# Block products for the short sequence's gate columns, with its normalised sums of x made early

## The chip, the core and the metric

The kernel runs on one core of a Trainium2 chip. The metric is the device time of one execution in microseconds. All matrix products are done on TensorE (PE) with each fp32 operand split in two parts, a high one and a low one, so that one logical product is three matmuls: high x high, high x low, low x high.

## The reference, cut to what matters

Two sequences, one of 1024 tokens (the short one, sequence 0) and one of 2048 (the long one, sequence 1, worked on in two chunks of 1024), get 16 meta tokens in front and pass through one encoder layer. What matters here is the input projection and what is made of its gate columns:

```python
xn = _rmsnorm(h, g_pre)                  # one norm per token
proj = xn @ w_in + b_in                  # 1024 -> 6672 columns
na_q, na_k, na_v, na_z, ml_qk, ml_v, ml_z, ml_o, ml_g, mg = jnp.split(proj, SPLIT_IDX, axis=-1)
ya = (neighbourhood_attention(na_q, na_k, na_v) * silu(na_z)) @ w_a
yb = (mlstm(ml_qk, ml_v, ml_g, ml_o) * silu(ml_z)) @ w_b
ga, gb = jnp.split(jax.nn.sigmoid(mg), 2, axis=-1)      # the 2048 gate columns
y = (ga * ya + gb * yb) @ w_out
return h + _rmsnorm(y, g_post)
```

The gate columns `mg` are 16 blocks of 128 columns. They are needed only at the end, when the two branches are merged.

## The kernel before, in words

**Two streams of work, one order on PE.** `dense()` (L1993) yields the projections, and at the end the merge and output products, piece by piece, each with a planned cost in us: 0.235 for a matmul 512 wide, 0.12 for one 256 wide (L134). `sparse()` (L2038) yields the steps of the mLSTM and of the attention. `run()` (L2057) interleaves them: each sparse step names how much dense work is to stand beside it (L135: 0.965 for an attention step of the long sequence), and the dense generator is drawn on until that sum is used up. So PE's order is written out by hand; the other engines' order comes from a scheduler, apart from side work that is put behind the last evacuation.

**The dense order** is `PLAN` (L42). The short sequence's `m` columns (mLSTM), then its `n` and `v` columns (attention), then the long sequence's two chunks, then the `n` and `g` columns of both long chunks, then the short sequence's `g` columns, then six final blocks of 512 tokens (`final`, L1825): merge products, then output products. The sparse order is mLSTM 0, attention 0, mLSTM 1, attention 1.

**Direct columns.** A block of 128 columns for 512 tokens is 8 steps of k with three matmuls 128x512 each, 24 in all (`fm_half`, L707, and `mm3`, L199 to L204). Columns and tokens of a chunk of 1024 give 2 x 24 per block of columns. Three PSUM banks (`pj`) take such results in turn.

**Block products.** For the chunks in `SW` (L43, the two long chunks) the columns `n` and `g` are made in pairs of blocks: the 2 x 2 block product (two column blocks by two halves of tokens, with k split in two) is done with seven products instead of eight (`sgates`, L923). A product is 4 steps of k by three matmuls, 12 matmuls (L955 to L957). It needs sums and differences of the weight blocks (made by `wprep`, L567, and `nprep`, L600) and of blocks of x (made by `tprep`, L627), both split in two parts again and kept in DRAM. `tprep` reads x's two halves of tokens from SBUF, adds their parts, and writes four tiles of sums `t0` to `t3`; `tload` (L901) reads them back for `sgates`. While a chunk's sums are being loaded, its first two pairs are done as direct columns (`lead`, L835). In `sgates` three banks A, E, R change roles: ACT copies a bank into another (L972, L979) or into SBUF (L981), DVE adds such a copy to a bank (L985, L987), and the result goes to `fm_evac` (L657).

**Normalisation.** For the long sequence x is normalised when it is split (`build_half`, L466). For the short sequence it isn't: its projections start before the norms are known, and `fm_evac` multiplies each result by a row of norms `rr` on DVE (L669 to L672). `rr` is written to DRAM (L508) and read back in `gclose` (L899) for the gate columns much later. x of the short sequence, and of the long one's first chunk, is written to DRAM by a queue `xput` (`xkeep`, L540) and read back when its later columns come up.

**Side work.** `beside()` (L549) runs after each piece of dense work and counts these turns. It issues one write of `xput` at certain turns and advances each side generator at every n-th turn: `wprep` at every 3rd, at every 6th from its last two pairs on; `tprep` of the first long chunk at every 4th from the start of that chunk's `m` columns; `tprep` and `nprep` of the second at every 2nd. What is left of a `tprep` is run down before the chunk's last group of columns (`group`, L1000). A turn is six matmuls 512 wide or twelve 256 wide.

**Buffers.** SBUF has a left pool that is `bp` in most stages (work tiles, such as four `xr` of 128x1024) and is exchanged for `gp` (the tiles `t1` to `t3`) in the stage of block products (`gopen`, L887, and `gclose`, L893). A final block loads its y tiles with a generator (`yload`, L1784) into the buffers of x, and waits until the attention of its 512 tokens is done.

## Time and profile before

| | |
|---|---|
| runs of the kernel before | 2701.67 us median of 3 (2700.21 to 2706.63) |
| the profiled execution | 2705.33 us, of which 2703.3 is the span of the trace |
| mean granted clock of TensorE | 0.995 |
| matmuls | 16000 |
| bytes moved by DMA | 783.72 MB |

Times in the profile are those of one execution, counted from the start of its span. PE is TensorE's matmuls, PEld its weight loads, DVE the vector engine, ACT the scalar engine, POOL GpSimd, SP the queue that issues nearly all DMAs. Matmuls are pipelined: the next one starts before the last has ended, so durations add up to more than the busy time. In a group's row, the last part tells how long the engine had been idle just before these instructions and what ended most of it.

### The profile page before, as it was taken

What the parts mean: (1) busy time and instruction counts of PE and PEld (TensorE: products, weight loads), DVE (VectorE), ACT (ScalarE), POOL (GpSimd) and SP (SyncE); (2) the same over time, 40 slices, a digit from 0 to 9 for tenths busy, and PEclk for the clock granted to TensorE, in tenths of its full rate; (3) what the DMA queues carried; (4) which work ended last, traced back from release to release, by engine and by line L of the source; (5) the groups of instructions that cost most, each with busy time, mean ns of one, the idle gap of its engine ahead of it and who ended that gap; (6) DMA issues with size and microseconds to landing.
All of it is one profiled execution on the core that took longest, in us unless ns stands there. A gap on an engine that the chain in (4) does not pass through costs nothing.

```text
span 2703.3 us, 47407 instructions
## 1 busy us (share of the span) xinstructions
PE 2658.4 (98%) x16000; PEld 2345.6 (87%) x16000; DVE 1910.4 (71%) x5234; ACT 1418.5 (52%) x3350; POOL 17.4 (1%) x100
## 2 busy tenths in 40 slices
PE   9999998999999999999999999999999999999998
PEld 7898897789987999878888888888889888989888
DVE  5444687978648888446866767658478989897954
ACT  6322555565345654356655566555355655656521
POOL 0000000000000000000000000000000000000000
PEclk9999998999999999999999999999999999999999
DMA  9988887899986898798889988895769798998965
GB/s 373 344 323 316 306 302 277 295 348 345 317 270 228 295 349 298 248 305 259 262 288 329 368 288 258 282 344 189 219 221 303 250 312 257 309 294 262 333 230 202
DMA packets 405986, 783.72 MB, mean 290 GB/s; under 512 B 51472, under 2 KB 180448, under 8 KB 404208
## 3 DMA queue, kind: packets, MB, share of 16 engines
q1 hardware_dynamic: 404624, 778.01, 85.6%
q0 software_dynamic: 1120, 2.69, 0.4%
q8 instruction: 127, 2.08, 0.3%
q14 instruction: 115, 0.94, 0.1%
HBM read 531.66 MB, written 248.88 MB: 289 GB/s over the span
## 4 chain that ended last, share of the span: by engine, by line
PE 70%; DVE 6%; DMA 5%; ACT 2%; issue 1%; SPq 0%; DVEq 0%; ACTq 0%
PE pj L202 8%; PE pj L203 8%; PE pj L204 8%; PE pj L955 6%; PE pj L957 6%; PE pj L956 6%; PE pj L1898 3%; PE pj L1899 3%; PE pj L1900 3%; PE pj L762 3%; PE pj L763 3%; PE pj L764 3%; PE sm L1247 2%; PE tr L1232 2%; DMA stk<-nq 1%
## 5 line engine op out<-in xcount | busy, mean ns | idle before, releaser
L202 PE MATMUL pj<-xh,whi 128*128 128x512 f32 (+1 forms) x992 | 385.5, 389 | 2.7 <-ACT st L679 1.5
L203 PE MATMUL pj<-xl,whi 128*128 128x512 f32 (+1 forms) x992 | 375.3, 378 | 0.1
L204 PE MATMUL pj<-xh,wlo 128*128 128x512 f32 (+1 forms) x992 | 374.7, 378 | 0.2 <-DVE wlo L304 0.2
L762 PE MATMUL pj<-whi,xh 128*128 128x256 f32 (+1 forms) x1152 | 329.7, 286 | 0.0
L763 PE MATMUL pj<-wlo,xh 128*128 128x256 f32 (+1 forms) x1152 | 325.0, 282 | 0.6 <-DMA wlo<-wl 0.6
L764 PE MATMUL pj<-whi,xl 128*128 128x256 f32 (+1 forms) x1152 | 324.7, 282 | 0.0
L204 PEld LDWEIGHTS pj<-xh,wlo 128*128 128x128 f32 x992 | 188.0, 189 | 37.3 <-DVE wlo L304 0.4
L1898 PE MATMUL pj<-whi,mh 128*128 128x256 f32 x768 | 219.6, 286 | 0.7 <-DMA whi<-wh 0.7
L763 PEld LDWEIGHTS pj<-wlo,xh 128*128 128x128 f32 x1152 | 217.0, 188 | 1.0 <-DMA wlo<-wl 0.8
L202 PEld LDWEIGHTS pj<-xh,whi 128*128 128x128 f32 x992 | 188.2, 190 | 33.8 <-ACT st L679 2.0
L762 PEld LDWEIGHTS pj<-whi,xh 128*128 128x128 f32 x1152 | 217.1, 188 | 0.2
L764 PEld LDWEIGHTS pj<-whi,xl 128*128 128x128 f32 x1152 | 217.0, 188 | 0.0
L1900 PE MATMUL pj<-whi,mlo 128*128 128x256 f32 x768 | 216.4, 282 | 0.0
L1899 PE MATMUL pj<-wlo,mh 128*128 128x256 f32 x768 | 216.3, 282 | 0.0
L203 PEld LDWEIGHTS pj<-xl,whi 128*128 128x128 f32 x992 | 188.4, 190 | 28.9 <-issue 1.0
L202 PE MATMUL pj<-yh,whi 128*128 128x512 f32 x384 | 154.1, 401 | 0.0
L203 PE MATMUL pj<-yl,whi 128*128 128x512 f32 x384 | 150.8, 393 | 0.8 <-DVE yl L1800 0.8
L204 PE MATMUL pj<-yh,wlo 128*128 128x512 f32 x384 | 151.2, 394 | 0.0
L1898 PEld LDWEIGHTS pj<-whi,mh 128*128 128x128 f32 x768 | 145.2, 189 | 1.8 <-DMA whi<-wh 0.9
L1899 PEld LDWEIGHTS pj<-wlo,mh 128*128 128x128 f32 x768 | 145.4, 189 | 0.9
L1900 PEld LDWEIGHTS pj<-whi,mlo 128*128 128x128 f32 x768 | 145.3, 189 | 0.0
L1239 DVE TENSOR_TENSOR pts<-tr,pts 96x384 fp32r<-96x384 f32 (+2 forms) x192 | 118.7, 618 | 32.8 <-ACT pts L1234 31.1
(368 smaller groups left out, 6739.2 us busy)
## 6 DMA issues: line engine op xcount, KB each, us to landing
whi<-wh SPq DMA_DIRECT2D x136, 512.0 KB
wlo<-wl SPq DMA_DIRECT2D x136, 512.0 KB
whi<-q SPq DMA_DIRECT2D x63, 512.0 KB
wlo<-q SPq DMA_DIRECT2D x55, 512.0 KB
wraw<-wu SPq DMA_DIRECT2D x48, 512.0 KB
gt<-st SPq DMA_DIRECT2D x96, 256.0 KB
tg<-gt SPq DMA_DIRECT2D x96, 256.0 KB
wh<-whi SPq DMA_DIRECT2D x36, 512.0 KB
```

Of the source, the lines that this page charges most:

```text
L202: mm(out, ah, bh, start=start, stop=False)
L203: mm(out, ah, bl, start=False, stop=False)
L204: mm(out, al, bh, start=False, stop=stop)
L762: nc.tensor.matmul(o, xh, wh, start=k == 0, stop=False)
L763: nc.tensor.matmul(o, xh, wl, start=False, stop=False)
L764: nc.tensor.matmul(o, xl, wh, start=False, stop=k == KT - 1)
L955: mm(bank, w[:, 0, k], xh[:, k], start=fresh and k == 0, stop=False, skip_group_check=True)
L956: mm(bank, w[:, 0, k], xl[:, k], start=False, stop=False, skip_group_check=True)
L957: mm(bank, w[:, 1, k], xh[:, k], start=False, stop=k == 3, skip_group_check=True)
L1898: nc.tensor.matmul(o, mh[:, k, xs], wh, start=clear > 0 and k == 0, stop=False)
L1899: nc.tensor.matmul(o, mh[:, k, xs], wl, start=False, stop=False)
L1900: nc.tensor.matmul(o, ml[:, k, xs], wh, start=False, stop=clear < 2 and k == KT - 1)
```

## The change

- `SW` now has the short sequence's chunk too: of its eight pairs of gate columns the first two stay direct, the other six are made by seven products each. The plan's order stays.
- The short sequence's block sums are made early, during its own `m`, `n` and `v` columns, from turn 34 on, one step at every 6th turn. There `tprep` adds the two parts of x, multiplies by `rr`, splits the normalised x again, writes it to DRAM (in place of the unnormalised x that `xput` wrote), and makes the sums from it. The gate columns are then not multiplied by `rr` at the evacuation, and `rr` is not kept in DRAM any more.
- `wprep` no longer splits and writes the weight block "21" of the six pairs that are no longer direct anywhere.
- `tprep` of the first long chunk begins at turn 370 and steps at every 3rd turn.
- `xput` (now of the long chunk alone) writes at every 3rd turn from the start.
- The last pair's `sgates` starts the y loads of the first final block; the left pool is reopened as `bp` after the short sequence's gate columns instead of ahead of them.
- Dense work beside an attention step of the long sequence: 0.93 instead of 0.965.

The core of the diff:

```diff
-SW = ((1, 0), (1, 1024))
+SW = ((0, 0), (1, 0), (1, 1024))
...
-A_N, A_D, A_A, A_G = (1.08, 0.965), 1.63, 1.79, 1.3
+A_N, A_D, A_A, A_G = (1.08, 0.93), 1.63, 1.79, 1.3
...
-            self.xkeep(s, 0, self.xs[0], NM)
-            self.xkeep(s, t0, x)
...
-                self.RD = self.dp.tile([P, D], F32, name="rrd")
-                nc.sync.dma_start(self.RD[:, :], self.rr.rearrange("p a t -> p (a t)"))
...
-        if self.xput and self.turn > 36 and self.turn % (6 if self.turn < 280 else 3) == 1:
+        if self.xput and self.turn % 3 == 1:
...
-                nc.scalar.activation(o[:, :, 0], raw[:, f], AF.Copy)
-                sub(o[:, :, 1], raw[:, f], o[:, :, 0].bitcast(F32))
-                for q, op in enumerate(ops):
+                c = slice(p > 7 and ops[0] == "21", 2)
+                nc.scalar.activation(o[:, c, 0], raw[:, f, c], AF.Copy)
+                sub(o[:, c, 1], raw[:, f, c], o[:, c, 0].bitcast(F32))
+                for q, op in list(enumerate(ops))[c]:
...
-    def tprep(self, s, t0):
+    def tprep(self, s, t0, after):
...
-        while len(self.xs) < 2:
+        while len(self.xs) < 2 or self.turn < after:
             yield
-        (h0, l0), (h1, l1) = self.xs
+        if s == 0:
+            for a in range(2):
+                self.xkept[s, t0 + 512 * a] = [dp.tile([P, KT, 512], F32, name=f"x{part}{s}_{t0 + 512 * a}") for part in "hl"]
+        halves = [[x[:, :, b:b + 512].bitcast(F32) for x in y] for y, b in zip(self.xs, (0 if s else NM, 0))]
         for e in range(4):
             ks = slice(2 * e, 2 * e + 2)
             r0, r1, ta, hi = [self.bp.tile([P, 2, 512], F32, name="xr", bufs=4) for _ in range(4)]
-            for r, h, l in ((r0, h0, l0), (r1, h1, l1)):
-                nc.vector.tensor_tensor(r, h[:, ks, :512].bitcast(F32), l[:, ks, :512].bitcast(F32), op=ALU.add)
+            for a, (r, (h, l)) in enumerate(zip((r0, r1), halves)):
+                tt(r, h[:, ks], l[:, ks], ALU.add)
+                if s == 0:
+                    tt(r, r, self.rr[:, a:a + 1].to_broadcast([P, 2, 512]), ALU.mult)
                 yield
+            if s == 0:
+                for a, r in enumerate((r0, r1)):
+                    nc.scalar.activation(hi.bitcast(F32R), r, AF.Copy)
+                    tt(ta.bitcast(F32R), r, hi)
+                    for d, x in zip(self.xkept[s, t0 + 512 * a], (hi, ta)):
+                        nc.sync.dma_start(d[:, ks, :], x)
+                    yield
...
-            if s == 0:
+            if s == 0 and col < C_GA:
...
-        self.rr = self.bp.tile([P, 2, 512], F32, name="rr", tag="gain", bufs=1)
-        self.nc.sync.dma_start(self.rr.rearrange("p a t -> p (a t)"), self.RD[:, :])
...
-            if end and nxt:
-                nx = [self.xload(*nxt)]
+            if end and nxt[0] == "f":
+                self.ystart(*nxt[1:])
+                next(self.ygen)
+            elif end:
+                nx = [self.xload(*nxt[:2])]
...
-        if sw:
-            last = t0 > 0
-            self.sides.append([chain(self.tprep(s, t0), self.nprep() if last else ()), 2 if last else 4])
-            side_ = self.sides[-1]
+        if sw and not reuse:
+            self.tside = chain(self.tprep(s, t0, 34 if s == 0 else 370 if t0 == 0 else 0), self.nprep() if t0 else ())
+            self.sides.append([self.tside, 6 if s == 0 else 2 if t0 else 3])
...
-            if last and sw:
-                for _ in side_[0]:
+            if last and sw and (nxt or t0):
+                for _ in self.tside:
                     pass
...
-                for cost in self.sgates(s, t0, cols, self.lead(j), nxt and nxt[:2]):
+                for cost in self.sgates(s, t0, cols, self.lead(j), nxt):
                     yield cost
                     self.beside()
+                    if self.y:
+                        next(self.ygen, None)
+                        next(self.ygen, None)
```

More of the change, by code (lines that the diff above doesn't have):

```diff
@@ L545, in xkeep @@
                 d = self.dp.tile([P, KT, 512], F32, name=f"x{part}{s}_{t0}")
-                self.xput.extend((d[:, k, :], x[:, k, base:base + 512].bitcast(F32)) for k in range(KT))
+                self.xput.extend((d[:, k, :], x[:, k, :512].bitcast(F32)) for k in range(KT))
                 self.xkept[s, t0].append(d)
@@ L575, in wprep @@
             if p == 12:
-                self.sides[0][1] = 6
+                [x for x in self.sides if x[0] is self.wside][0][1] = 6
             raw = pool.tile([P, 2, 2, 512], F32, name="pr", bufs=1)
@@ L625, in nprep @@
                 yield
-    def tprep(self, s, t0):
+    def tprep(self, s, t0, after):
         nc, dp = self.nc, self.dp
-        self.TD[s, t0] = [[dp.tile([P, 4, 512], F32, name=f"t{j}{part}{t0}") for part in "hl"] for j in range(4)]
+        tt = lambda o, a, b, op=ALU.subtract: nc.vector.tensor_tensor(o, a, b, op=op)
+        self.TD[s, t0] = [[dp.tile([P, 4, 512], F32, name=f"t{j}{part}{s}{t0}") for part in "hl"] for j in range(4)]
         td = self.TD[s, t0]
-        while len(self.xs) < 2:
+        while len(self.xs) < 2 or self.turn < after:
             yield
-        (h0, l0), (h1, l1) = self.xs
+        if s == 0:
+            for a in range(2):
+                self.xkept[s, t0 + 512 * a] = [dp.tile([P, KT, 512], F32, name=f"x{part}{s}_{t0 + 512 * a}") for part in "hl"]
+        halves = [[x[:, :, b:b + 512].bitcast(F32) for x in y] for y, b in zip(self.xs, (0 if s else NM, 0))]
         for e in range(4):
@@ L1016, in group @@
             last = j == len(jobs) - 1
-            if last and sw:
-                for _ in side_[0]:
+            if last and sw and (nxt or t0):
+                for _ in self.tside:
                     pass
-                self.sides = [x for x in self.sides if x is not side_]
+                self.sides = [x for x in self.sides if x[0] is not self.tside]
             if last and sw and t0:
```

14 lines of the change are left out of this document (7 added, 7 removed).

## The prediction

> **What bounds the kernel now.** I read four views in this order: the page's engine table, its chain that ended last, the table of busy time in stretches of 50 us, and the instructions in order of time.
>
> ```profile
> span 2703.3 us, 47407 instructions
> PE 2658.4 (98%) x16000; PEld 2345.6 (87%) x16000; DVE 1910.4 (71%) x5234; ACT 1418.5 (52%) x3350; POOL 17.4 (1%) x100
> ...
> DMA packets 405986, 783.72 MB, mean 290 GB/s; under 512 B 51472, under 2 KB 180448, under 8 KB 404208
> ...
> PE 70%; DVE 6%; DMA 5%; ACT 2%; issue 1%; SPq 0%; DVEq 0%; ACTq 0%
> ```
>
> PE is idle for only 2703.3 - 2658.4 = 44.9 us and holds 70% of the chain. So a matmul taken out shortens the run, and anything that adds PE idle time lengthens it. The stretches (columns: PE, PEld, DVE, ACT, POOL busy, granted clock, DMA share, GB/s) show where this holds:
>
> ```profile
> 100.00:150.00 50.00, 50.00 (x397) 49.30 (x396) 18.61 (x29) 13.36 (x18) 0.00 (x0) 1.00 0.88 319
> ...
> 300.00:350.00 50.00, 48.53 (x312) 43.88 (x311) 37.63 (x94) 28.75 (x72) 3.79 (x15) 1.00 0.95 338
> 350.00:400.00 50.00, 50.00 (x429) 50.00 (x428) 43.20 (x131) 28.18 (x70) 0.10 (x1) 1.00 0.86 294
> ...
> 500.00:550.00 50.00, 45.60 (x216) 37.75 (x215) 41.22 (x137) 25.83 (x64) 0.10 (x1) 0.93 0.81 281
> ...
> 600.00:650.00 50.00, 49.49 (x410) 49.27 (x410) 46.17 (x151) 26.36 (x66) 0.10 (x1) 1.00 1.01 345
> ...
> 1850.00:1900.00 50.00, 50.00 (x260) 42.28 (x259) 36.52 (x135) 23.55 (x63) 2.39 (x8) 1.00 0.50 166
> ...
> 1950.00:2000.00 50.00, 50.00 (x259) 42.03 (x258) 34.44 (x89) 29.89 (x67) 0.00 (x0) 1.00 0.58 176
> ...
> 2250.00:2300.00 50.00, 48.73 (x247) 40.40 (x246) 48.05 (x123) 25.96 (x59) 0.00 (x0) 1.00 0.89 277
> ```
>
> The short sequence's gate columns run from about 1796 to 2010 us. PE is full there, DVE has 30% and the DMA engines 42 to 50% to spare.
>
> **What a matmul is worth.** Multiplying by its listed duration is the trap here, so its row comes first, then starts of matmuls in the gate stage (the first pair, direct) and in the block products just before it (the second pair).
>
> ```profile
> L202 PE MATMUL pj<-xh,whi 128*128 128x512 f32 x824 | 337.0, 409 | 1.5 <-ACT st L679 1.5
> ```
> ```profile
> 1905.66 0.39 PE L202 MATMUL pj<-xh,whi 128*128 128x512 f32 x1
> ...
> 1911.91 0.39 PE L202 MATMUL pj<-xh,wlo 128*128 128x512 f32 x1
> ```
> ```profile
> 1788.15 0.39 PE L955 MATMUL pj<-xh,wlo 128*128 128x512 f32 x1
> ...
> 1793.68 0.39 PE L955 MATMUL pj<-xh,wlo 128*128 128x512 f32 x1
> ```
>
> One lasts about 0.39 to 0.41 us, but the next starts long before it ends: 27 matmuls lie between the first pair, 6.25 / 27 = 0.2315 us each, and 24 between the second, 5.53 / 24 = 0.2304. Spacing, not duration, is what PE's time is made of.
>
> The Trainium skill, "TensorE: Matmul & The Clock Gate", section "Wait — 56ns, not 53.3ns?", gives warm starts N / 2.4 GHz + 2.5 ns apart, 215.7 ns for N = 512. By that figure the 72 matmuls counted below would be worth 15.5 us; this trace's spacing is 7% wider, and the trace decides.
>
> **The change part by part.**
>
> *Removed from PE.* Of the eight pairs of gate columns (16 columns of 128), the first two stay direct: 2 pairs x 2 columns x 2 halves x 8 k-steps x 3 = 192 matmuls. The other six were 6 x 2 x 2 x 24 = 576 and become 6 pairs x 7 products x 12 = 504. That is 72 fewer, 576 x 0.2315 - 504 x 0.2304 = 133.3 - 116.1 = 17.2 us by the two spacings, or 72 x 0.231 = 16.6 by their mean. I take **-16.7 us**.
>
> *The gate stage around it.* The 32 products with the row of norms at the evacuation go (DVE, 0.70 us each, 22 us in all); 12 sums and 18 copies of a bank come.
>
> ```profile
> L672 DVE TENSOR_TENSOR pj<-pj,rr x88: 415/699/700, 26.9 to 2008.7; 128x512 f32<-128x512 f32 x67, 128x248 f32<-128x248 f32 x11, 128x264 f32<-128x264 f32 x10
> ```
> ```profile
> L985 DVE TENSOR_TENSOR st<-pj,st 128x512 f32<-128x512 f32 x26 | 17.9, 687 | 10.6 <-PE pj L957 7.2 <-DMA wlo<-q3s 3.3
> L979 ACT ACTIVATE pj<-pj 128x512 f32<-128x512 f32 x26 | 15.1, 582 | 22.4 <-PE pj L957 22.4
> ```
> ```profile
> PE pj L955 <- ACT pj L972: 1.4, 2, 0.7
> PE pj L202 <- ACT st L679: 1.5, 1, 1.5
> ```
>
> DVE's balance here is 12 x 0.69 - 22 = -14 us; ACT gains 18 x 0.58 = 10 us beside PE. In the 26 pairs that already run this way the bank copies held PE for 1.4 us in two waits, both on the first copy of a chunk, so one more chunk costs about 0.7. All three banks are in use in this scheme, and a bank copy has to be done within one product (12 x 0.2304 = 2.8 us), where direct columns leave two banks spare. The 26 pairs ran mostly beside the mLSTM; these six run mostly beside the attention, for which no row exists. Bounds 0 and 6 x 1.5 = 9 (the longest wait of a dense matmul for ACT, once a pair); I take +1, near the 0.7.
>
> *Data.* Six more units of DMA appear: block sums of x, 32 writes of 256 KB (8 MB) and 8 MB read back; weights, 25 units of 1 MB where there were 16, so +9 MB; six 0.5 MB weight blocks are no longer written. The sum is about +22 of 784 MB. The read-back and the weights fall into the gate stage with its DMA share of 0.50 to 0.58: I count 0. If that cover were gone, an extra 17 MB at 290 GB/s would be 59 us of transfers, spread over some 200 us.
>
> *Sums of the short x, made early.* One step every sixth turn of the dense stream from turn 36; 36 steps end at turn 246. Counting turns by the columns' yields, these are about 65 and 372 us. The steps issue, by the rows below: DVE 8 sums, 8 scalings, 8 splits and 4 wide lows at 1.22, and 16 block sums and 8 narrow lows at 0.68, together 28 x 1.22 + 24 x 0.68 = 50 us; ACT 12 x 1.06 + 8 x 0.63 = 18 us; SP 48 issues where the old write-back of x had 32.
>
> ```profile
> L639 DVE TENSOR_TENSOR xr<-xh,xl x16: 1210/1218/1226, 496.2 to 904.0; 128x1024 f32<-128x1024 f32 x16
> L641 DVE TENSOR_TENSOR xr<-xr x8: 681/684/694, 504.7 to 911.0; 128x512 f32<-128x512 f32 x8
> L649 ACT ACTIVATE xr<-xr x24: 611/627/1060, 529.6 to 924.6; 128x512 fp32r<-128x512 f32 x16, 128x1024 fp32r<-128x1024 f32 x8
> ```
>
> A step is 1.4 us of DVE in 8 us. At 100 to 150 us DVE is at 37% and takes that unseen. At 350 to 400 it is at 86% and the last three steps still come, so the cover ends there. Behind a step that waits for its buffer's write to land stand the evacuations, and for those the matmuls; with three banks a direct column outlasts about 2 x 24 x 0.231 = 11 us. The longest such hold on the chain now is:
>
> ```profile
> 841.45 7.05 DMA t1h<-xr
> ```
>
> That is under 11, so I take 0, with a bound of one full PE stall above (6.8, priced next).
>
> *Sums of the long x, moved later.* Their 28 steps (per quarter 9 DVE and 3 ACT instructions and 8 writes) begin at turn 370, about 590 us, instead of near 490, and are moved past the write-back of the long x and the weight preparation on SP. What they leave is a stall:
>
> ```profile
> 496.17 1.21 DVE L639 TENSOR_TENSOR xr<-xh,xl 128x1024 f32<-128x1024 f32 x1
> ...
> 498.23 1.22 DVE L639 TENSOR_TENSOR xr<-xh,xl 128x1024 f32<-128x1024 f32 x1
> ...
> 504.65 0.68 DVE L641 TENSOR_TENSOR xr<-xr 128x512 f32<-128x512 f32 x1
> ...
> 509.06 0.45 PE L202 MATMUL sm<-v,sh 128*128 128x130 f32 x1 [4.40 <-DVE num L1688]
> ```
> ```profile
> 510.00:515.00 5.00, 5.00 (x16) 4.01 (x16) 4.97 (x25) 2.26 (x7) 0.05 (x1) 0.62 0.42 129
> 515.00:520.00 5.00, 5.00 (x27) 4.22 (x26) 4.86 (x19) 3.53 (x9) 0.05 (x1) 1.00 0.43 162
> ```
>
> PE waits 4.40 us for an mLSTM result that DVE reaches late, and three of these sums (3.1 us) stand in DVE's line ahead of it. Then the granted clock is 0.62 for a stretch: 16 matmuls in place of 27, about 2.4 us lost. So one such stall is 4.4 + 2.4 = 6.8 us. Without the three sums the wait would be 1.3 us and the clock might stay up: 3.1 + 2.4 = 5.5 won. The other bound is 0: what is late next is the mLSTM's own line on DVE, 82% busy there. I take **-3**. Where the steps go, at 600 to 650 us, DVE is at 92% and the DMA share 1.01, but about as many of the same steps are there already: 0 to +1, taken as 0.
>
> The Trainium skill, the same page, section "What's actually happening", says that the PE clock halves after an idle window of about 3.4 us and needs a busy one to return. The 4.40 us wait and the 0.62 behind it agree; the rule speaks against this change wherever it makes a new wait of that length.
>
> *Pace and end.* The attention's dense filler falls from 0.965 to 0.93 per step; with 541 steps that is 18.9 of the planner's us against 72 x 0.235 = 16.9 of filler that no longer exists. It matters:
>
> ```profile
> L1264 DVE TENSOR_TENSOR yg<-yg,zt x24: 671/681/693, 843.3 to 2591.8; 128x512 f32<-128x512 f32 x24
> ...
> L203 PE MATMUL pj<-yl,whi x64: 387/390/504, 2603.3 to 2647.8; 128*128 128x512 f32 x64
> ```
>
> The short stretch between the last attention product (2591.8) and the last block's first matmul (2603.3) is one store, one load and one split: the end now hangs on the attention and on the dense stream alike. With 16.7 us less dense work and the old pace, dense would be there at 2586.6, before the attention had ended, and PE would wait. With the new pace the attention ends 18.9 x 0.231 / 0.235 = 18.6 us sooner too, near 2573, and the gap is kept. I count 0; if the attention couldn't be pressed together the whole gain would go (a rival below).
>
> *Small edits, one answer.* The row of norms is no longer stored and reloaded (two 0.5 MB transfers), half of ACT's and DVE's share of six weight blocks goes (6 x 0.6 us each), and the left pool is reopened after these columns, just ahead of the last product blocks: their first gate loads can then wait for the block sums' last reader, one product (2.8 us) before the end, while two spare banks give 5.5 us. 0, with a bound of +2.
>
> **Sum.** -16.7 (matmuls) + 1 (bank copies) - 3 (the stall) = -18.7 us. The profiled execution took 2705.3 (2703.3 of span and 2.0 around it), so 2686.6; it lies 3.7 above the median 2701.67 of the runs shown, so on that scale the forecast is **2683**.
>
> **Rivals.** (Times on the scale of the median.)
>
> *More is won.* The 4.4 us stall goes with its slow stretch and the copies cost nothing: -17.2 - 6.8, 2678. For it: 3.1 of the 4.4 us are named above. Against: the rest of DVE's line is still there.
>
> *Less is won.* The bank copies, now beside the attention's ACT work, hold PE by 1.5 us a pair, and the stall stays: -16.7 + 9, 2694. For it: the slack of one product, and PE idle 1.3 us at 2250 to 2300 with DVE at 96%. Against: PE at 100% in all of 1850 to 2000 with the attention already there.
>
> *The pace doesn't hold.* DVE at 96% (2250 to 2300) can't bring the attention to an end sooner; the last block starts at 2603 as now, and only the stall's 3 us are won: 2699. Against: DVE is at 96% in a few stretches only, and pressing the attention's 541 steps into 18.6 of some 715 us less raises its share by under 3%.
>
> *Slower.* The place is 300 to 408 us, where the short sequence's mLSTM begins and DVE is already at 75 to 86%. If the early sums slip, because a step waits for its buffer's write, their steps of 1.4 us in 8 (17%) lie on top of 86% and DVE is full; each mLSTM step that comes 4 us late then costs 6.8 us, as at 509. Three of them give 20.4 and undo the gain; five give 34: -16.7 + 1 - 3 + 34, 2717. It decides from a slip of about ten turns, 15 us, on. For it: waits like this already occur when x is built beside this mLSTM:
>
> ```profile
> 460.09 0.55 PE L1648 MATMUL sc<-q,kh 128*128 128x256 f32 x1 [4.31 <-DVE nwy L166]
> ```
>
> Against: 33 of the 36 steps are due before 350 us, where DVE has 25% or more to spare.
>
> A reading of 72 x 0.394 = 28.4 us, by duration, would give 2673; the spacing rules it out.
>
> **How the numbers follow.** Forecast 0.58, more 0.12, less 0.14, pace 0.08, slower 0.08. A measurement of this kernel can tell about 0.3% from no change, which is 8.1 us: faster means under 2693.6. The forecast and "more" lie below it, "less" sits on the line and is split 0.08 to 0.06, "pace" is within. Faster 0.78, same 0.14, slower 0.08. The range takes the forecast, "more" and "less" with some play beyond them, 2674 to 2697; the two cases above it are 0.16 together.
>
> **What would show it.** Right: 15928 matmuls in place of 16000; the group of 128x512 direct products down by 576 and the block products up by 504, with spacing still 0.231; PE's busy time down by about 17 us and its idle time no higher than 44.9; no sums of x between 480 and 590 us and a shorter wait, or a clock of 1.00, near 509; the last attention product near 2573 and the last block's first matmul 10 to 15 us behind it. Wrong: PE waits for ACT's bank copies of more than 1 us in the gate stage, stretches with the clock under 1.00 between 300 and 420, DVE waits for the writes of the block sums, or a wait of PE ahead of the last block. If matmul busy time fell by 17 us and the span didn't, the lost time must stand in one of these waits.

## The result

The changed kernel takes **2713.85 us** (median of 20 runs, 2704.46 to 2721.22), the kernel before 2702.64 in 20 runs beside it (2696.68 to 2712.44): a ratio of 1.0038, 95% interval 1.0028 to 1.0048. It is 11.2 us slower where 18.7 us of gain were forecast, and it lies above the range. The profiled execution took 2712.26 us, with a mean granted clock of 0.992 (0.995 before). The head of its page:

```profile
span 2710.5 us, 47460 instructions
PE 2645.7 (98%) x15928; PEld 2334.1 (86%) x15928; DVE 1937.3 (71%) x5266; ACT 1440.0 (53%) x3388; POOL 16.9 (1%) x100
...
DMA packets 411652, 805.75 MB, mean 297 GB/s; under 512 B 52016, under 2 KB 180992, under 8 KB 409104
...
PE 84%; DMA 6%; DVE 6%; ACT 2%; issue 1%; SPq 1%; DVEq 0%; ACTq 0%
```

The work did go: 72 matmuls fewer and 12.7 us less of PE's busy time (matmuls at half clock count as longer, and about 41 us of the span are at half clock where it was 25). But PE's idle time rose from 44.9 to 2710.5 - 2645.7 = 64.8 us, and the DMAs grew by 22 MB, as counted. The stretches that answer to those shown of before (PE, PEld, DVE, ACT, POOL, granted clock, DMA share, GB/s), and in a second block two of the kernel before, from 450 and 1900 us on:

```profile
300.00:350.00 50.00, 46.02 (x293) 41.59 (x292) 40.46 (x92) 27.86 (x68) 3.31 (x14) 0.97 0.91 324
450.00:500.00 50.00, 40.74 (x187) 33.66 (x187) 41.86 (x107) 36.34 (x85) 0.30 (x3) 0.86 0.92 326
500.00:550.00 50.00, 48.88 (x246) 40.74 (x246) 42.53 (x137) 29.65 (x72) 0.10 (x1) 1.00 0.84 286
1900.00:1950.00 50.00, 46.85 (x219) 38.31 (x218) 17.81 (x59) 17.43 (x33) 2.38 (x8) 1.00 0.90 246
1950.00:2000.00 50.00, 50.00 (x246) 41.76 (x245) 28.53 (x77) 29.70 (x64) 0.00 (x0) 0.97 0.87 278
```
```profile
450.00:500.00 50.00, 45.69 (x214) 37.85 (x214) 42.64 (x103) 33.84 (x79) 0.20 (x2) 0.93 0.94 350
...
1900.00:1950.00 50.00, 50.00 (x230) 40.92 (x229) 22.07 (x63) 15.90 (x30) 0.00 (x0) 1.00 0.71 218
```

Read the third row of the change first: between 500 and 550 us PE is at 48.9 with a clock of 1.00, where before it had 45.6 and 0.93, so the stall at 505 us is gone as forecast. The loss is in the rows around it. At 450 to 500 PE has 40.7 us in place of 45.7 and a clock of 0.86 in place of 0.93, at 300 to 350 it has 46.0 in place of 48.5, and in the gate stage, at 1900 to 2000, the DMA share is 0.90 and 0.87 where it was 0.71 and 0.58. The longest waits of PE (what waits, on what; us in all, times, longest):

```profile
PE sc L1658 <- DVE q L1612: 12.4, 2, 11.0
...
PE tr L1789 <- DVE hb L1784: 3.2, 1, 3.2
PE pj L963 <- ACT pj L990: 3.2, 1, 3.2
```

The order of matmuls on PE is the same in both kernels up to the short sequence's gate columns, so each matmul can be compared with itself. By the time of the kernel before, after minus before is -1.6 us at 116 us, +6.5 at 338, +11.3 at 418, +17.8 at 447, +5.1 at 542, +14.5 at 888 and +16.9 at 1804, just ahead of the gate columns. So it is lost before the changed products run, in two places: up to 470 us, of which 5.1 us are left at 542, since the kernel before has stalls of its own in between, and between 542 and 888. In the second place PE waits 3.0 us for ACT at 792, and 2.8 and 2.3 us for DVE at 835 and 839, with a slow stretch behind the first and the last; DVE is busy for all of 830 to 835 there, while the DMA share is 0.14. After 1804 the change wins 9.7 us back, down to the 7.2 by which the two spans differ, though three more stalls (1945, 2006 and 2025 us) stand there.

**The stall at 448 us.** Instructions in order of time on PE, with what the engine waited for in brackets, then those of ACT and DVE ahead of it:

```profile
447.84 0.39 PE L204 MATMUL pj<-xh,wlo 128*128 128x512 f32 x1
459.26 0.58 PE L1658 MATMUL sc<-q,kh 128*128 128x256 f32 x1 [11.02 <-DVE q L1612]
```
```profile
446.26 0.42 ACT L1638 ACTIVATE v<-va 128x260 fp32r<-128x260 f32 x1 [4.11 <-DMA va<-mv]
```
```profile
453.38 3.49 DVE L531 TENSOR_TENSOR xl<-xt,xh 128x1024 fp32r<-128x1024 f32 x3
...
457.65 1.21 DVE L567 TENSOR_TENSOR po<-pr,po 128x1024 fp32r<-128x1024 f32 x1
458.79 0.41 DVE L1612 TENSOR_TENSOR q<-cv,q 128x256 fp32r<-128x256 f32 x1
```

DVE is the engine named, and it is busy; but it started late. Ahead of it, ACT sat idle for 4.11 us until a load of the mLSTM (`va<-mv`) had landed. The splits of the long x (L531) then stand ahead of the one product that PE needs. The chain that ended last shows how far back this goes (start, us, what):

```profile
387.26 5.38 DMA t3h<-xr
...
394.52 4.67 DMA q<-whi
...
413.71 7.66 DMA xt<-xt
...
425.08 5.53 DMA va<-mv
...
434.92 5.77 DMA wraw<-wu
440.75 5.48 DMA va<-mv
```

In 59 us, up to 446, the chain passes through these six transfers and one stretch of PE, 9 us from 403.6 on. The first of them is a write of the block sums that the change makes early (`t3h`).

**The stall at 1945 us.** ACT, then PE, in the changed kernel:

```profile
1943.15 0.63 ACT L1177 ACTIVATE qB<-stk 64x512 fp32r<-64x512 f32 x1 [5.35 <-DMA stk<-nq]
...
1947.86 0.57 ACT L990 ACTIVATE pj<-pj 128x512 f32<-128x512 f32 x1
```
```profile
1948.48 0.50 PE L963 MATMUL pj<-xh,wlo 128*128 128x512 f32 x1 [3.15 <-ACT pj L990]
```

The long attention begins here. ACT's first instruction for it waits 5.35 us for the attention's first load, and the bank copy of the new products stands behind that in ACT's line. From its issue to its first use the load takes 7.9 us (1935.2 to 1943.2); in the kernel before it takes 4.7 (1916.9 to 1921.6).

### The profile page after: what moved, and what is told of

Its sections match the earlier page's. It is cut to its first block, busy times and chain, and to the rows that moved or that the text cites. A ratio compares the mean times of both kernels' runs of the same rounds, so it can differ in the third digit from the quotient of the medians.

```text
span 2710.5 us, 47460 instructions
## 1 busy us (share of the span) xinstructions
PE 2645.7 (98%) x15928; PEld 2334.1 (86%) x15928; DVE 1937.3 (71%) x5266; ACT 1440.0 (53%) x3388; POOL 16.9 (1%) x100
## 4 chain that ended last, share of the span: by engine, by line
PE 84%; DMA 6%; DVE 6%; ACT 2%; issue 1%; SPq 1%; DVEq 0%; ACTq 0%
PE pj L202 9%; PE pj L203 9%; PE pj L204 9%; PE pj L963 7%; PE pj L965 7%; PE pj L964 7%; PE pj L772 4%; PE pj L774 4%; PE pj L773 4%; PE pj L1908 3%; PE pj L1910 3%; PE pj L1909 3%; PE sm L1257 2%; PE tr L1242 2%; DMA xt<-xt 1%
## 5 line engine op out<-in xcount | busy, mean ns | idle before, releaser
L202 PE MATMUL pj<-xh,whi 128*128 128x512 f32 (+1 forms) x896 | 346.3, 387 | 2.0 <-ACT whi L303 2.0
L203 PE MATMUL pj<-xl,whi 128*128 128x512 f32 (+1 forms) x896 | 337.9, 377 | 0.1
L204 PE MATMUL pj<-xh,wlo 128*128 128x512 f32 (+1 forms) x896 | 337.6, 377 | 0.3 <-DVE wlo L304 0.3
L204 PEld LDWEIGHTS pj<-xh,wlo 128*128 128x128 f32 x896 | 170.4, 190 | 33.2 <-DVE wlo L304 0.5
L202 PEld LDWEIGHTS pj<-xh,whi 128*128 128x128 f32 x896 | 170.8, 191 | 30.4 <-ACT whi L303 2.9
L203 PEld LDWEIGHTS pj<-xl,whi 128*128 128x128 f32 x896 | 170.8, 191 | 26.7 <-issue 1.0
L1244 ACT ACTIVATE pts<-tr 96x384 fp32r<-96x384 f32 (+2 forms) x192 | 103.2, 538 | 86.9 <-PE tr L1242 86.4
```

The lines of the kernel that those rows point to most:

```text
L202: mm(out, ah, bh, start=start, stop=False)
L203: mm(out, ah, bl, start=False, stop=False)
L204: mm(out, al, bh, start=False, stop=stop)
```

## The experiments

**Theories.** The loss up to 470 us comes with the block sums made early. Theory A: their steps on DVE and ACT crowd the start of the mLSTM, as the rival "Slower" has it. Theory B: their 32 writes do it, by their bytes on the DMA engines (B1), or by their place in SyncE's queue, ahead of loads (B2). For the gate stage: the bank copies don't cost by themselves, but the start of the attention beside them does. Rivals to these: the later sums of the long x, and the new pace. The difference from the kernel before is taken as the ratio times 2703.

**The early sums alone.** The changed kernel with direct gate columns, the old pace, and the sums of the long x where they were; the early sums are written and not used, and all weight blocks are written as before. The core of the edit:

```diff
-A_N, A_D, A_A, A_G = (1.08, 0.93), 1.63, 1.79, 1.3
+A_N, A_D, A_A, A_G = (1.08, 0.965), 1.63, 1.79, 1.3
+SWG = ((1, 0), (1, 1024))        # for the products, in place of SW
...
-            self.tside = chain(self.tprep(s, t0, 34 if s == 0 else 370 if t0 == 0 else 0), self.nprep() if t0 else ())
+            self.tside = chain(self.tprep(s, t0, 34 if s == 0 else 0), self.nprep() if t0 else ())
```

> The short sequence's block sums are made early as in the changed kernel, and its gate columns read the normalised x, but these columns stay direct (no products saved, old pace 0.965, long chunk's sums at their old place); the sums are written and not used. Theory (three places pay: the early sums, the second long chunk's entry, the gate stage): matched matmuls of the two profiles lie 11 to 18 us apart by 450 us, so this kernel loses 8 to 14 us against before, 2711 to 2717. Rival (the early sums are hidden, all is lost in the gate stage): within 3 us of before, 2700 to 2706.

Measured 2721.84 us (2716.95 to 2725.19), ratio 1.0072, interval 1.0060 to 1.0084. The early sums cost about 19 us by themselves. It follows too what the rest of the change brings on top of them, the products with the moved sums of the long x and the new pace: 2721.84 - 2713.85 = 8.0 us, where 16.7 were counted for the products alone.

**The later sums of the long x alone**, put into the kernel before:

```diff
-        while len(self.xs) < 2:
+        while len(self.xs) < 2 or self.turn < after:
...
-            self.sides.append([chain(self.tprep(s, t0), self.nprep() if last else ()), 2 if last else 4])
+            self.sides.append([chain(self.tprep(s, t0, 0 if last else 370), self.nprep() if last else ()), 2 if last else 3])
```

> The kernel before with one edit: the first long chunk's sums begin at turn 370 and step at every 3rd turn. Theory: the stall at 505 us goes (-6.8) and the second long chunk's entry, at 750 to 850 us, comes to stand behind the late sums (+9.8 in the matched matmuls): before +3, 2703 to 2708. Rival (the later sums only gain, the entry is late for another reason): 2695 to 2698.

Measured 2703.86 us (2696.06 to 2707.49), ratio 1.0006, interval 0.9997 to 1.0015. Its trace has no stall at 505 us any more, and yet the time stays: the forecast -3 us isn't there. The matched matmuls of this trace show where it goes: 6.2 us are won between 500 and 520, and 5.0 are lost again between 700 and 888.

**The change without that shift:**

```diff
-            self.tside = chain(self.tprep(s, t0, 34 if s == 0 else 370 if t0 == 0 else 0), self.nprep() if t0 else ())
-            self.sides.append([self.tside, 6 if s == 0 else 2 if t0 else 3])
+            self.tside = chain(self.tprep(s, t0, 34 if s == 0 else 0), self.nprep() if t0 else ())
+            self.sides.append([self.tside, 6 if s == 0 else 2 if t0 else 4])
```

> The changed kernel with the first long chunk's sums back at their old place (at once, every 4th turn). Theory: the entry's 9.8 us come back and the stall of 6.8 us at 505 returns: 3 us below the changed kernel, 2708 to 2713. Rival (the shift is a pure gain): 5 to 7 us above it, 2719 to 2721.

Measured 2710.65 us (2700.03 to 2719.12), ratio 1.0022, interval 1.0007 to 1.0037, which overlaps with the whole change. The shift is neither the loss nor a gain that can be told. In this kernel's trace too the matched matmuls lose between 542 and 888 (+6.9 to +14.1 us), in that of the early sums alone they don't (+10.6 to +11.2): what costs there isn't found by these runs.

**The change with the old pace:**

```diff
-A_N, A_D, A_A, A_G = (1.08, 0.93), 1.63, 1.79, 1.3
+A_N, A_D, A_A, A_G = (1.08, 0.965), 1.63, 1.79, 1.3
```

> The changed kernel with the old pace, 0.965 of dense work beside an attention step. Theory (the pace is needed and innocent): dense reaches the last block ahead of the attention's end and PE waits there, 5 to 12 us more than the changed kernel, 2719 to 2726. Rival (the denser attention is what costs the gain): 3 to 7 us less, 2707 to 2711.

Measured 2713.82 us (2711.89 to 2719.49), ratio 1.0046, interval 1.0034 to 1.0058: no different. Its wait of PE between 2600 and 2625 us shows what the new pace avoids, at the start of the last block:

```profile
PE pj L202 <- ACT yh L1826: 5.3, 1, 5.3
```

**The early sums sooner**, at every 3rd or 4th turn, so that they end well ahead of the mLSTM's start:

```diff
-            self.sides.append([self.tside, 6 if s == 0 else 2 if t0 else 3])
+            self.sides.append([self.tside, 3 if s == 0 else 2 if t0 else 3])     # the second kernel: 4
```

> The changed kernel with the short sequence's sums stepped at every 3rd turn in place of every 6th, so that they end near 212 us, before the short sequence's mLSTM begins at 247. Theory A (the early sums cost 19 us because their DVE and ACT steps stand in line ahead of the mLSTM's first steps, 290 to 420 us): 12 to 19 us below the changed kernel, 2695 to 2702. Theory B (their writes crowd the DMA queues): 16 MB now go out in half the time, so no gain, 2710 or more.

> The same with every 4th turn, sums ending near 262 us. Theory A: nearly as much is won, 8 to 18 us, 2696 to 2706. Theory B: 2710 or more.

Measured 2713.27 us (2702.39 to 2714.77), ratio 1.0026, interval 1.0012 to 1.0040, and 2716.08 us (2707.81 to 2722.63), ratio 1.0046, interval 1.0028 to 1.0064. By the traces the last of the steps begins at 273.5 and 268.8 us, later than expected but well ahead of the 383.0 of the change. PE still stalls at 295 (3.1 us) and 312 us (6.6) in the first of the two, where no such step runs any more. So it isn't steps beside the mLSTM: theory A falls.

**The early sums without their 32 writes;** everything else as in the first kernel of this series.

```diff
-                    for d, x in zip(td[j], (a, b)):
+                    for d, x in zip(td[j], (a, b)) if s else ():
```

> The kernel with early sums and direct gate columns (2721.8) without the writes of the sums t0 to t3, which it doesn't use: 32 of the 48 writes and 8 MB fewer, DVE and ACT as they were. Theory A: no change, 2718 to 2725. Theory B: most of the 19 us comes back, 2703 to 2710.

Measured 2703.37 us (2700.09 to 2707.88), ratio 1.0002, interval 0.9993 to 1.0012. The whole cost is gone while DVE's and ACT's steps are all there. In this kernel theory B holds. PE's waits between 250 and 350 us, with the writes and then without:

```profile
PE tr L1530 <- DVE kf L1494: 8.1, 2, 4.4
PE sm L1380 <- DVE g_eT L1382: 0.4, 1, 0.4
```
```profile
PE sc L1659 <- DVE q L1613: 2.4, 1, 2.4
PE sm L1380 <- DVE g_eT L1382: 0.7, 1, 0.7
```

`kf` is made from a load of the mLSTM (`raw<-mk`). SyncE's queue in order of time, with the writes and then without:

```profile
277.96 0.82 SPq L332 DMA_DIRECT2D q<-whi  x2
278.88 0.40 SPq L709 DMA_DIRECT2D nq<-st  x1
279.37 1.00 SPq L332 DMA_DIRECT2D q<-wlo  x2
280.43 0.63 SPq L275 DMA_DIRECT2D wraw<-wu  x1
281.16 0.58 SPq L664 DMA_DIRECT2D t2h<-xr  x1
281.84 0.43 SPq L664 DMA_DIRECT2D t2l<-xr  x1
...
286.46 0.61 SPq L1408 DMA_DIRECT2D raw<-mk  x1
```
```profile
274.00 0.76 SPq L1408 DMA_DIRECT2D raw<-mk  x1
...
278.12 1.12 SPq L332 DMA_DIRECT2D q<-whi  x2
```

The matmuls of both kernels run at the same time up to here (291 us: 0.2 us apart), but the load is issued at 286.46 with the writes and at 274.00 without: it stands behind a round of weight transfers and two writes of sums, where otherwise it stood ahead of that round. Its transfer then takes 6.42 us in the chain that ended last, and the product that needs it comes at 296.8, 3.7 us late. The kernel pins only PE's order of instructions (`build`); that of the other queues is worked out when the kernel is built, and an added DMA moves it. This is one stall of the kernel with the early sums alone: in the change itself that load goes out at 277.56 us, and the matched matmuls show no loss at 297 (+1.8 us, as at 280).

**Why the writes cost.** Seven edits to the kernel with the early sums alone or to the whole change. The first three: the writes on GpSimd's queue in the whole change; half the rows of each write; half of the writes (the upper parts only).

```diff
-                        nc.sync.dma_start(d[:, e, :], x[:, q] if len(js) > 1 else x)
+                        (nc.sync if s else nc.gpsimd).dma_start(d[:, e, :], x[:, q] if len(js) > 1 else x)
...
+                        n = P if s else 64
+                        nc.sync.dma_start(d[:n, e, :], x[:n, q] if len(js) > 1 else x[:n])
...
+                    for d, x in list(zip(td[j], (a, b)))[:2 if s else 1]:
```

> The changed kernel, with the 32 early writes of the short sequence's block sums put on GpSimd's DMA queue in place of SyncE's; bytes, packets and the steps on DVE and ACT stay. Theory B1 (the writes cost because their 8 MB take time of the 16 DMA engines in stretches with a share of 0.9, so that the mLSTM's loads land later): the bytes are the same, so the time stays near the changed kernel's 2713.85, 2709 to 2718, and PE's waits between 290 and 470 us stay. Theory B2 (the writes cost because they stand ahead of those loads in SyncE's queue): the loads are issued as before, most of the 19 us come back, 2695 to 2701.

> The kernel with the early sums alone (gate columns direct, old pace), in which each of the 32 writes of the block sums takes 64 of its 128 rows: 4 MB less, but as many issues on SyncE at the same places and behind the same results; the sums are unused here. Without the writes it took 2703.4, with all of them 2721.8. B1 (bytes on the DMA engines): about half of the 18 us goes, 2712, 2709 to 2715. B2 (issues standing in SyncE's queue): nothing goes, 2719 to 2724.

> The kernel with the early sums alone, in which only the upper parts of the block sums are written: 16 whole writes of 256 KB, 4 MB, the same bytes as with half the rows (2717.1, 32 writes) but half the issues; DVE's and ACT's steps stay, the sums are unused here. Bytes alone (B1): as with half the rows, 2712 to 2717. Issues alone (B2): half of the 18.4 us between 2703.4 (no writes) and 2721.8 (all 32), 2712.6. Both, each with a share: below either single halving, 2706 to 2711.

The other four, like the two just before with the early sums alone and the sums unused: all writes on GpSimd's queue; each write issued twice; one row of 128 in each write; parts of x that have long been ready in place of the sums.

```diff
+                        (nc.sync if s else nc.gpsimd).dma_start(d[:, e, :], x[:, q] if len(js) > 1 else x)
...
+                        if s == 0:
+                            nc.sync.dma_start(self.twice[j][x is b][:, e, :], x[:, q] if len(js) > 1 else x)
...
+                        n = P if s else 1
+                        nc.sync.dma_start(d[:n, e, :], x[:n, q] if len(js) > 1 else x[:n])
...
+                        ready = halves[q][x is b][:, 2 * e]
+                        nc.sync.dma_start(d[:, e, :], (x[:, q] if len(js) > 1 else x) if s else ready)
```

> The kernel with the early sums alone, all 32 writes of 256 KB on GpSimd's DMA queue; bytes and steps stay, the sums are unused here. B1 (bytes): 2718 to 2724, as with the writes on SyncE (2721.8). B2 (place in SyncE's queue): near 2703.4, as without writes, 2702 to 2707. Both: some 5 us less than 2721.8 as in the changed kernel, 2714 to 2718.

> The kernel with the early sums alone, each of the 32 writes issued twice, the second time to a tensor that nobody reads: 64 writes, 16 MB. If the DMA engines are full in these stretches (B1), every further MB costs its whole transfer: 18.4 us for the first 8 MB, 8.4 MB at the best rate that a slice shows (some 410 GB/s) = 20 us for the next, 2742, 2736 to 2750. If only the place in the queue behind a step counts, the second of two writes issued back to back adds little: 2722 to 2730.

> The kernel with the early sums alone, in which each of the 32 writes of the block sums takes one row of 128 (2 KB instead of 256 KB): as many issues on SyncE behind the same results, nearly no bytes; the sums are unused here. If bytes and what they delay are the price (B1): as without writes, 2703.4, 2700 to 2707. If the issues and their waits in SyncE's queue are (B2): as with half the rows or more, 2712 to 2721.

> The kernel with the early sums alone, in which the 32 writes of 256 KB take parts of x that have been in SBUF for long in place of the sums: same bytes, same number of issues at the same steps, but no write waits for a step's result, and no buffer of the sums is held until a write lands; the sums are unused here. B1 (bytes): 2718 to 2724, as with the sums (2721.8). B2 (waits in the queue) or buffers held: 2703 to 2710.

| kernel with the early sums alone | bytes | median, us | ratio (95%) | over before, us |
|---|---|---|---|---|
| no writes | 0 | 2703.37 | 1.0002 (0.9993 to 1.0012) | 0.5 |
| 32 writes of 2 KB | 0.06 MB | 2709.61 | 1.0024 (1.0015 to 1.0033) | 6.5 |
| 16 writes of 256 KB | 4 MB | 2710.20 | 1.0024 (1.0012 to 1.0035) | 6.5 |
| 32 writes of 128 KB | 4 MB | 2717.10 | 1.0050 (1.0037 to 1.0063) | 13.5 |
| 32 of 256 KB, GpSimd's queue | 8 MB | 2714.09 | 1.0033 (1.0021 to 1.0045) | 8.9 |
| 32 of 256 KB, data ready before | 8 MB | 2716.58 | 1.0050 (1.0037 to 1.0064) | 13.5 |
| 32 of 256 KB, as in the change | 8 MB | 2721.84 | 1.0072 (1.0060 to 1.0084) | 19.5 |
| 64 of 256 KB | 16 MB | 2726.16 | 1.0080 (1.0068 to 1.0093) | 21.6 |

On GpSimd's queue the whole change takes 2708.44 us (2704.17 to 2713.45), 1.0020 (1.0010 to 1.0029).

Neither B1 nor B2 holds alone. With 32 issues in SyncE's queue the cost is 6.5, 13.5 and 19.5 us at 0.06, 4 and 8 MB, so about a third is there nearly without bytes and the rest grows with them. It falls again when the issues leave that queue (8.9) or are half as many (6.5). With ready data it is 13.5, whose interval just overlaps that of the sums. What speaks against a simple sum is the last row: twice the bytes and issues add nothing that can be told. The order in the queues changes with these edits. The mLSTM's first load goes out at 274.0 to 274.1 us without writes, with one row, with half the rows and with half the writes; at 279.3 with the writes on GpSimd's queue; and at 285.1 to 286.5 with whole writes of the sums, of ready data, and doubled. That late load is thus one part of the price, and not all of it: half the rows cost 13.5 us with the load in its old place. And in the kernel with a step at every 3rd turn, whose last write goes out at 274.8 us, the load stands behind weights and loads of x until 285.0. The runs don't separate a byte from the order that it brings; that stays open. Shown is that in this kernel the writes cost it all, and that fewer and smaller ones cost less.

**The start of the attention.** The whole change with its long attention's first loads issued 17 turns ahead of their first use, in place of 6, and the pace adjusted for the dense work so used:

```diff
-A_N, A_D, A_A, A_G = (1.08, 0.93), 1.63, 1.79, 1.3
+A_N, A_D, A_A, A_G = (1.08, 0.911), 1.63, 1.79, 1.3
...
-                for _ in range(2 if k else 17 - 11 * s):
+                for _ in range(2 if k else 17):
```

> The changed kernel with 17 instead of 6 dense steps between the long attention's first loads and its first instructions, and the pace 0.911 so that the attention's whole filler stays the same. Theory (in the gate stage ACT waits 5 us for the attention's first load with a bank copy behind it, and PE for the copy, 3.2 us and a slow stretch): 3 to 5 us below the changed kernel, 2709 to 2711. Rival (the hold comes from elsewhere or moves): 2712 to 2716.

Measured 2703.94 us (2698.73 to 2712.58), ratio 1.0001, interval 0.9990 to 1.0011: 9.9 us less than the whole change. PE's waits between 1780 and 2030 us in the change, and with the longer lead:

```profile
PE pj L963 <- ACT pj L990: 3.2, 1, 3.2
PE sm L1257 <- ACT prb L1225: 2.7, 1, 2.7
PE sm L1210 <- DVE sm L1234: 1.7, 1, 1.7
```
```profile
PE pj L963 <- ACT pj L1002: 0.5, 1, 0.5
PE sm L1257 <- ACT prb L1225: 0.5, 1, 0.5
PE pj L203 <- DMA xl<-xl: 0.2, 1, 0.2
```

7.6 us of waits become 1.2, with the bank copies and their number as they were. So it is the attention's late load, not the copies; the rest of the 9.9 us isn't shown wait by wait. The execution in this trace is the slowest of the twelve, 2712.58 us: the waits are gone in it, the gain in time isn't seen in it. All the traces together show it better. From the matmul at 1800 us (by the time of before) to the end of the span, the seven kernels with the products and the old lead win 2.9 to 9.7 us on the kernel before, and the three with the longer lead (this one and two below) 11.7 to 14.8.

**A version that uses both.** The early sums are written once as plain fp32 (16 writes, 4 MB) and split where they are read, in the gate stage, which also takes 24 steps off DVE and ACT early and halves the read-back; then the same with the longer lead; then that with its writes on GpSimd's queue.

```diff
-                nc.scalar.activation(a.bitcast(F32R), b, AF.Copy)
-                tt(b.bitcast(F32R), b, a)
+                if s:
+                    nc.scalar.activation(a.bitcast(F32R), b, AF.Copy)
+                    tt(b.bitcast(F32R), b, a)
                 for q, j in enumerate(js):
-                    for d, x in zip(td[j], (a, b)):
+                    for d, x in zip(td[j], (a, b)) if s else ((td[j][1], b),):
...                                               # tload, where s == 0
+                        for k in range(0, 4, 2):
+                            self.nc.scalar.activation(hi[:, k:k + 2], lo[:, k:k + 2].bitcast(F32), AF.Copy)
+                            self.nc.vector.tensor_tensor(lo[:, k:k + 2], lo[:, k:k + 2].bitcast(F32), hi[:, k:k + 2].bitcast(F32), op=ALU.subtract)
```

> The changed kernel, with the block sums of the short sequence written once as plain fp32 (16 writes, 4 MB in place of 8, and 4 MB read back), and split into their two parts where they are read, in the gate stage (8 ACT copies and 8 DVE subtractions of 128x1024 there, 12 ACT and 12 DVE steps fewer early). Under B1 and B2 alike half of the writes' 19 us goes, -9; the gate stage's splits lie beside matmuls and its read-back is halved, 0 to -5: 2702, 2698 to 2707. If the time stays at 2713, the cost isn't one of the writes' number or bytes (contrary to the run without them), or the splits cost at the attention's start what the writes gave.

> The same with the longer lead between the long attention's first loads and their first use (17 turns, pace 0.911), which alone took the changed kernel from 2713.9 to 2703.9. If the two costs are separate (the early writes between 290 and 470 us, the attention's start beside the gate columns at 1945 to 2025), the gains add: 2713.9 - 10 - 9 = 2695, 2691 to 2700, which would be below the kernel before (2702.6) by 0.3%. If they are one cost given back twice, 2701 to 2705.

> The unsplit sums with the longer lead (2691.3), with their 16 early writes on GpSimd's DMA queue. In the changed kernel the same move of 32 writes gave 5.4 us. If the rest of the early cost is in SyncE's queue, half of that comes, 2688 to 2690; if it is bytes alone, 2691, 2689 to 2694.

Measured: unsplit 2702.73 us (2697.45 to 2708.29), 0.9999 (0.9989 to 1.0008). With the lead **2691.32 us** (2687.59 to 2698.36), 0.9962 (0.9948 to 0.9976). With GpSimd's queue as well 2696.75 us (2692.68 to 2700.22), 0.9969 (0.9957 to 0.9981), no better. The two remedies add up (11.1 and 9.9 us alone, 22.5 together), so the two costs are separate. The second kernel is quicker than both kernels of this case, by 10.3 us against before. The head of its page:

```profile
span 2688.1 us, 47409 instructions
...
PE 2644.5 (98%) x15928; PEld 2331.4 (87%) x15928; DVE 1936.2 (72%) x5262; ACT 1441.2 (54%) x3384; POOL 16.9 (1%) x100
```

PE is as busy as in the changed kernel (2644.5 to 2645.7 us) and idle for 43.6 us in place of 64.8: 10.3 of the 16.7 us counted for the matmuls that were taken out now show in the time.

## Why the prediction was wrong

- **The step that failed: "Data", with "Sums of the short x, made early", "so I take 0".** The prediction counted the 32 writes of 256 KB among the bytes, priced the read-back and the weights, and gave the writes no term. With the gate columns direct they cost 18.5 us (2721.84 with, 2703.37 without). The steps on DVE and ACT that make them were priced at 0, and that was right: +0.5 us, not to be told from 0.
- **Why it was missed.** The rows for it had been quoted: a DMA share of 0.88 at 100 to 150 us and 0.95 at 300 to 350, and 48 issues on SP against 32. The prediction asked only whether DVE had room there, and whether a step waits for its own buffer. It didn't ask which load stands behind the added issue on SyncE and who waits for it. The bound, "one full PE stall above" (6.8), was too small by nearly a factor of three: up to 350 us alone, PE waits twice with the writes (8.1 us in all) for a product made from a load of the mLSTM. Whether the bytes or the changed order cost more stays open.
- **The second failed step: "The gate stage around it", +1 us.** It cost about 9: the products brought 8.0 us (2721.84 to 2713.85) in place of 16.7, and a longer lead for the attention gave 9.9 back. That is the size of its upper bound, 9 us, but not its mechanism: not "a bank copy has to be done within one product", since the copies stayed in that run, but a bank copy queued on ACT behind an instruction that waits for a load. That load met a DMA share of 0.90, with the read-back and the weights that the prediction had put at 0 by rows of 0.50 and 0.58. Those were two of the four stretches of the gate stage: in the kernel before, the share is 0.90 at 1800 to 1850 and 0.71 at 1900 to 1950, just where the attention's first load falls, so the cover wasn't there. That the load was late for this reason is argued; that an earlier issue mends it is shown.
- **Right: the matmuls.** 576 direct ones fewer and 504 in products more, 15928 in all, and still 0.231 us apart (23 spacings in 5.31 us, from 1939.62 on). Their worth in time isn't measured alone: PE's busy time fell by 12.7 us where 17 was the sign, and the version in which both costs are reduced takes 10.3 us less than before.
- **Right in sight, not in time: the stall at 505 us.** It went, with its slow stretch; but the shift alone gives 1.0006 (0.9997 to 1.0015), so the -3 us isn't there. In the trace of that kernel 5.0 of the 6.2 us won are lost again between 700 and 888; the prediction had taken the steps' new place as 0 and hadn't looked at what follows it.
- **The pace:** the wait of 5.3 us ahead of the last block with the old pace is the one that was foreseen. With the stream late anyway it didn't change the time (2713.82). The attention was to end near 2573; its last product stands at 2595.4, since everything came 16.9 us late to the gate columns and the three stalls followed. The last block's first matmul with `yl` is 14.8 us behind it:

```profile
L1274 DVE TENSOR_TENSOR yg<-yg,zt x24: 666/680/693, 856.8 to 2595.4; 128x512 f32<-128x512 f32 x24
```
```profile
2610.21 0.40 PE L203 MATMUL pj<-yl,whi 128*128 128x512 f32 x1
```

- **The rival "Slower"** had the place (300 to 408 us, and on to 460), the kind of loss (stalls with half clock behind them) and came near in size, 2717, by luck. Its mechanism was wrong: it was to decide by a slip of the steps on a full DVE, and steps that end about 110 us earlier changed nothing that can be told, while without the writes all the steps cost nothing.

By terms: +0.5 for the early steps, +18.5 for their writes (both by the runs without and with them) and -8.0 for all the rest, in all +11; measured 11.2. That the -8.0 are -16.7 for the matmuls and about +9 for the attention's start is a split that closes by construction; its one check is the 9.9 us of the longer lead. The loss between 542 and 888 lies somewhere in these terms and has no run of its own.

## What to carry to other kernels

A DMA that an edit adds is an instruction in a queue as well as bytes, and it can move the loads behind it: here 32 writes cost 18.5 us of a kernel whose PE is busy for 98%. Before such a DMA is put at nothing, look at the DMA share where it is issued, name the next loads of that queue and the engine that waits for each. Write intermediate results once, in the smallest form, and split or derive them where they are read, if that stage has room (11.1 us here). And when an engine gets new work that PE depends on, look for an instruction ahead of it in that engine's line that waits for a load, and issue that load earlier (9.9 us here). And look at every stretch of a stage before its cover is counted on, not at the two emptiest.

## What the runs showed of the hardware

TensorE's clock fell to half after shorter waits than the 4.40 us of the prediction's stall. Two waits of the changed kernel are of only 1.8 us, with small matmuls of 36x36 before and behind it, and 2.0 us, with one of 0.6 us and a single matmul just ahead of it (PE's waits between 270 and 280, and between 308 and 320 us):

```profile
PE sm L1379 <- DVE g_eT L1381: 1.8, 1, 1.8
```
```profile
PE sm L203 <- DVE vwl L1510: 2.0, 1, 2.0
```

The granted clock was 0.70 in the 5 us around the end of the first and just behind the second (sixth of the numbers behind the span of the row):

```profile
275.00:280.00 5.00, 3.22 (x11) 2.28 (x10) 2.04 (x7) 1.37 (x7) 0.00 (x0) 0.70 0.54 194
...
315.00:320.00 5.00, 5.00 (x32) 4.98 (x32) 3.39 (x10) 1.37 (x4) 0.00 (x0) 0.70 0.92 312
```

(1 - 0.70) x 5 / 0.5 = 3 us of each stretch were at half clock. A wait of 2.1 us at 2225 us of the kernel before left it at 1.00. The Trainium skill, "TensorE: Matmul & The Clock Gate", section "What's actually happening", has the clock halve after an idle window of about 3.4 us; by these rows a single wait of about half that can be enough, and needn't be.
